# Where the squares of the input's norm stand in the first stage of a hybrid decoder block

## The chip, the cores and the metric

One core of one Trainium2 chip runs the whole kernel in one launch. The metric is the device time in microseconds (us); three runs of the kernel before give a median of 1648.81 us (1648.59 to 1650.45).

## What is computed

A decoder block of 256 tokens and 2048 channels: a mixer (gated linear attention beside causal pooling, merged by gates), a cross-attention into 256 memory tokens and a gated MLP with a causal convolution, each behind a root-mean-square norm and with a residual. All is float32. Only the start of the mixer matters here:

```python
def rms_norm(x, g):
    xf = x.astype(jnp.float32)
    y = xf * lax.rsqrt(jnp.mean(xf * xf, axis=-1, keepdims=True) + EPS)
    return (y * g.astype(jnp.float32)).astype(x.dtype)
...
    proj = h @ w_in
...
    v = heads(proj[..., OFF_V:OFF_R], GLA_HV)
...
    gate_pre = (proj[..., OFF_A:OFF_P] @ w_a2 + b_a).astype(f32)
```

where h is rms_norm(x, g_mix). The kernel multiplies by the gain first, does the products, and puts the norm's factor (one number per token) on the results.

## The kernel before

Channels lie on the partitions, in 16 chunks of 128, and the 256 tokens in the free dimension. A float32 product is made of three products of rounded operands: each operand is split in a high part (a cast to fp32r on ScalarE) and a low part (operand minus high part, on VectorE), and high x high, low x high and high x low are added up in PSUM. For weights the split is L110 (`wh`, `wl`), five buffers each, from six buffers of raw tiles that SyncE's queue loads (L78). For the input, `split_gain` (L241 to L245) scales chunk c with the gain: `h.hi(c)` on ScalarE (L243) and `h.lo(c)` on VectorE (L244).

The program begins with eight products of constants (L356), and then the projection of the values and of the decay's inputs (`va_unit`, L386 to L405). It has two halves, n = 0 (heads 0 and 1) and n = 1 (heads 2 and 3), each of six units j with 2 or 3 chunks (the table VA). For a chunk there are 2 heads x 2 halves of the tokens x 3 products (L403, L404, L405), each 260 columns wide (256 values, 4 decay inputs): 12 a chunk and 192 a half. The sums of a half stand in four PSUM tiles `va`; those of n = 0 come from the pool mm, those of n = 1 from the pool aux (four tiles each).

Transfers of the input and of the first weight pieces are issued in turn (the table FIRST, L193, and L204 to L209): chunk 0, a weight piece, chunk 1, two pieces, chunk 2, and so on; from chunk 4 on two chunks a transfer. The loop at L361 emits the splits in the same turn, and `in_order` ties each split behind the one before, so that the scheduler that orders the program keeps this sequence on ScalarE and VectorE.

The norm needs the sum of squares of each token. `Sum.add` (L262) squares a chunk on ScalarE (L265 for the first, else L260) and adds it to an accumulator (L268): even chunks to `s_mix` on VectorE, odd ones to `s_mix2` on GpSimd. The squares of a chunk are emitted one turn after its split, tied behind it (L364, L365). After the first half the two accumulators are added (L417), two products with a column of ones give the sum per token (`cols`, L274) in an aux tile of their own, `root` (L288 to L297) makes the factor `rc`, and `rows` (L277) spreads it over the partitions after unit (1, 2). `va_out` (L407) takes the results of a half out of PSUM with that factor, after each half. Calls through `behind` stand after the last product emitted so far.

Of the kernel before, what the change touches and what calls it, by code (L numbers as in the profile page):

```python
# [8 lines left out]
F32 = mybir.dt.float32  # L9
# [6 lines left out]
P = 128  # L16
# [126 lines left out]
def block(ctx, tc, xT, memT, vecs, masks, wa2, wpool, w_va, w_in, w_branch, w_out, w_ckv_k, w_ckv_v, w_cq, w_co, w_up, w_down, out):  # L143
# [11 lines left out]
    aux = ctx.enter_context(tc.tile_pool(name="aux", bufs=4, space=PS))  # L155
# [30 lines left out]
    def xc(c):  # L186
        return x[c // 4][:, c % 4, :]
# [7 lines left out]
    def in_turn(pieces):  # L195
        pieces = iter(pieces)
        for n in FIRST:
            if isinstance(n, tuple):
                yield n, None
            else:  # L200
                for _ in range(n):
                    yield None, next(pieces)
# [21 lines left out]
    def col(base, c):  # L224
        return vec[:, base + c : base + c + 1]
# [3 lines left out]
    def behind(f, *args):  # L229

        with tc.issue_after(pe["last"].ins):
            return f(*args)

    def in_order(made, f):

        with ExitStack() as stack:
            for ins in made or ():
                stack.enter_context(tc.issue_after(ins.ins))
            return f()

    def split_gain(src, act, c, base):  # L241
        return (
            nc.scalar.activation(act.hi(c), src, AF.Identity, scale=col(base, c)),  # L243
            nc.vector.scalar_tensor_tensor(act.lo(c), src, col(base, c), act.hi(c).bitcast(F32), ALU.mult, ALU.subtract),  # L244
        )  # L245
# [5 lines left out]
    class Sum:  # L251
# [15 lines left out]
            sq, a = self.square(src)  # L267
            return a, self.eng.tensor_add(self.acc, self.acc, sq)  # L268

        def cols(self):  # L270

            ps = aux.tile([P, 2], F32, tag="aux", name=f"cps_{self.name}")
            for t in range(2):
                nc.tensor.matmul(ps[:, t : t + 1], lhsT=self.acc[:, t * P : (t + 1) * P], rhs=ones[:, 0:1], start=True, stop=True)  # L274
            return root(ps, 2, self.name)
# [12 lines left out]
    def root(ps, n, name):  # L288

        v, y, z, r = (const.tile([P, n], F32, name=f"rc{i}_{name}") for i in range(4))  # L290
        nc.vector.tensor_scalar(v, ps, 1.0 / D, EPS, ALU.mult, ALU.add)
        nc.scalar.activation(y, v, AF.Sqrt)
        nc.vector.reciprocal(y, y)
        nc.vector.tensor_mul(z, y, y)
        nc.vector.scalar_tensor_tensor(z, z, -0.5, v, ALU.mult, ALU.mult)
        nc.vector.scalar_tensor_tensor(r, z, 1.5, y, ALU.add, ALU.mult)
        return r  # L297
# [13 lines left out]
    def gemm(unit, act, name, n=NC):  # L311

        ps = mm.tile([P, 2 * T], F32, tag="mm", name=f"ps_{name}")
        products(ps, terms(W.get(unit), act, n))
        return ps
# [36 lines left out]
    h = Act(big, NC, "h")  # L352

    ones_ps = aux.tile([P, P], F32, tag="aux", name="warm")
    for i in range(8):
        nc.tensor.matmul(ones_ps, lhsT=ones, rhs=ones, start=True, stop=True)  # L356


    s_mix, s_mix2 = Sum("mix"), Sum("mix2", nc.gpsimd)
    made, late = None, []  # L360
    for chunks, piece in in_turn([f for j in range(6) for f in W.pieces(va0 + j)]):  # L361
        if piece:
            made = in_order(made, piece)
        for c in late:  # L364
            in_order(made, lambda: (s_mix, s_mix2)[c % 2].add(xc(c)))  # L365
        late = range(*chunks) if chunks else ()
        for c in late:
            made = in_order(made, lambda: split_gain(xc(c), h, c, V_MIX))

    def const_loads():  # L370
        nc.sync.dma_start(mask, masks[:, 0 : N_MASK * P].rearrange("p (n i) -> p n i", i=P))
        nc.sync.dma_start(wa, wa2)

        for t in range(16):
            nc.gpsimd.memset(inv_f[:, t : t + 1], 1.0 / (t + 1))
# [8 lines left out]
    va_ps = {}  # L384

    def va_unit(n, j):  # L386

        if j == 0:
            for hd in (2 * n, 2 * n + 1):
                pool, tag = (aux, "aux") if n else (mm, "mm")  # L390
                va_ps[hd] = [pool.tile([P, 260], F32, tag=tag, name=f"va{hd}_{t}") for t in range(2)]
        wps = W.get(va0 + len(VA) * n + j)
        first, end = VA[j]
        for c in range(first, end):
            for i in range(2):
                at = 2 * (c - first) + i
                hi, lo = wps[at // (end - first)]
                at = at % (end - first) * 260
                wh, wl = hi[:, at : at + 260], lo[:, at : at + 260]
                for t in range(2):  # L400
                    ps = va_ps[2 * n + i][t]
                    xh, xl = h.hi(c)[:, t * P : (t + 1) * P], h.lo(c)[:, t * P : (t + 1) * P]
                    nc.tensor.matmul(ps, lhsT=xh, rhs=wh, start=c == 0, stop=False)  # L403
                    nc.tensor.matmul(ps, lhsT=xl, rhs=wh, start=False, stop=False)  # L404
                    pe["last"] = nc.tensor.matmul(ps, lhsT=xh, rhs=wl, start=False, stop=c == NC - 1)  # L405

    def va_out(hd):  # L407
        for t in range(2):
            ps, r = va_ps[hd][t], rc[:, t : t + 1]
            nc.scalar.activation(v[t][:, hd, :], ps[:, 0:T], AF.Identity, scale=r)  # L410
            nc.vector.tensor_scalar(a_sb[:, t, 4 * hd : 4 * hd + 4], ps[:, T : T + 4], r, None, ALU.mult)

    for n in range(2):
        for j in range(len(VA)):
            va_unit(n, j)
            if (n, j) == (0, len(VA) - 1):
                nc.vector.tensor_add(s_mix.acc, s_mix.acc, s_mix2.acc)  # L417
                rc = behind(s_mix.cols)
                const_loads()
            if (n, j) == (1, 2):  # L420
                rB = behind(s_mix.rows, rc, mm)
        for i in range(2):
            va_out(2 * n + i)

# [233 lines left out]
    for m in range(NC):  # L660
        wps = W.get(br0 + m)
        ys = []
        for n in (1, 0):
            ps = mm.tile([P, 2 * T], F32, tag="mm", name=f"br{m}_{n}")
# [34 lines left out]
    for m in range(NC):  # L699
        ps = gemm(ck0 + m, me, f"ck{m}")  # L700
# [10 lines left out]
    for g in range(4):  # L711
        acc = [mm.tile([P, 512], F32, tag="mm", name=f"cv{g}_{t}") for t in range(2)]
        for j in range(4):
            wps = W.get(cv0 + 4 * g + j)
            for k in range(4):
                hi, lo = wps[k // 2]
                wh, wl = hi[:, (k % 2) * 512 : (k % 2 + 1) * 512], lo[:, (k % 2) * 512 : (k % 2 + 1) * 512]
                c = 4 * j + k
# [11 lines left out]
    qa, ka, va, pa, pts = {}, {}, {}, {}, {}  # L730
# [58 lines left out]
    for i in range(16):  # L789
        query(i // 4, i % 4)  # L790
        hd = i // 4 - 1
# [124 lines left out]
    for m in range(NC - TAIL, NC):  # L916
        pool, tag = (aux, "aux") if m >= NC - 2 else (mm, "mm")
        ps = pool.tile([P, 2 * T], F32, tag=tag, name=f"ps_dt{m}")
# [69 lines left out]
```

## Time and profile before

| | us |
|---|---|
| median of three runs | 1648.81 |
| the profiled execution's own time | 1650.06 |
| its span | 1648.3 |
| TensorE busy in the span | 1635.4 |
| VectorE busy | 1227.9 |
| ScalarE busy | 899.4 |
| GpSimd busy | 31.1 |

The span is what the profiler saw between the first and the last instruction; the own time also holds what lies around it. PE is TensorE, DVE is VectorE, ACT is ScalarE, POOL is GpSimd, SP is SyncE, whose queue issues the transfers; a q behind the name is an engine's instruction queue. A row of a timeline begins with its start and its length in us and ends with the idle time before it and what ended that.

### The profile page before, as it was taken

How to read it: one execution, taken by the hardware profiler on the slowest of the kernel's cores; microseconds unless marked ns; L12 is line 12 of the kernel's file. 1: busy time of each engine (PE TensorE's matmuls, PEld its weight loads, DVE VectorE, ACT ScalarE, POOL GpSimd, SP SyncE). 2: the span in 40 equal slices, each digit the busy share in tenths (PEclk: the TensorE clock that was granted, in tenths of full speed). 3: DMA queues.
4: the chain of work that ended last, by engine and by line, in shares of the span. 5: the costliest groups of instructions: out<-in, count | busy, mean ns of one | idle time of the engine just before them, and what ended most of it. 6: DMA issues, size and time to landing. Idle time of an engine off the chain costs nothing.

```text
span 1648.3 us, 26006 instructions
## 1 busy us (share of the span) xinstructions
PE 1635.4 (99%) x9900; PEld 1474.9 (89%) x9900; DVE 1227.9 (74%) x1906; ACT 899.4 (55%) x1376; POOL 31.1 (2%) x137
## 2 busy tenths in 40 slices
PE   8999999999999999999999999999999999999997
PEld 8999998989988898889999999999999999999987
DVE  7588768677888855447777788886678887678876
ACT  7555447445556644446555565654356664446563
POOL 2000000000001100000000000000000000000000
PEclk9999999999999999999999999999999999999999
DMA  8665556656666666665446666666666666666663
GB/s 275 208 200 171 168 166 189 218 169 201 195 220 210 196 199 196 192 194 177 154 144 199 194 195 200 196 200 196 199 196 198 198 196 200 195 201 194 180 183 109
DMA packets 90734, 316.15 MB, mean 192 GB/s; under 512 B 10208, under 2 KB 11104, under 8 KB 90608
## 3 DMA queue, kind: packets, MB, share of 16 engines
q1 hardware_dynamic: 90464, 314.43, 61.2%
q8 instruction: 77, 1.26, 0.3%
q14 instruction: 49, 0.40, 0.1%
q10 hardware_dynamic: 144, 0.05, 0.0%
HBM read 312.35 MB, written 2.10 MB: 191 GB/s over the span
## 4 chain that ended last, share of the span: by engine, by line
PE 97%; DMA 1%; DVE 1%; ACT 1%; issue 0%; SPq 0%; DVEq 0%; ACTq 0%
PE ps_up L329 19%; PE ps_up L330 10%; PE ps_g L329 7%; PE ps_dn L329 7%; PE ps_dn L330 4%; PE ps_g L330 4%; PE ps_wc L329 3%; PE ps_ck L329 3%; PE ps_cq L329 3%; PE br L329 3%; PE ps_wo L329 3%; PE ps_cq L330 2%; PE br L330 2%; PE ps_wc L330 2%; PE ps_ck L330 2%; PE cv L722 2%
## 5 line engine op out<-in xcount | busy, mean ns | idle before, releaser
L110 ACT CAST wh<-raw 128x1024 fp32r<-128x1024 f32 (+3 forms) x602 | 613.1, 1021 | 652.4 <-issue 204.1
L110 DVE TENSOR_TENSOR wl<-raw,wh 128x1024 fp32r<-128x1024 f32 (+3 forms) x602 | 718.2, 1195 | 331.9 <-ACT wh L110 322.2
L329 PE MATMUL ps_up<-h,wh 128*128 128x512 f32 x1408 | 469.9, 380 | 0.0
L330 PE MATMUL ps_up<-h,wl 128*128 128x256 f32 x1408 | 386.4, 274 | 0.0
L329 PEld LDWEIGHTS ps_up<-h,wh 128*128 128x128 f32 x1408 | 264.3, 188 | 45.3
L330 PEld LDWEIGHTS ps_up<-h,wl 128*128 128x128 f32 x1408 | 264.5, 188 | 0.0
L329 PE MATMUL ps_g<-h,wh 128*128 128x512 f32 x512 | 173.3, 384 | 0.0
L329 PE MATMUL ps_dn<-ga,wh 128*128 128x512 f32 x512 | 170.8, 380 | 0.0
L330 PE MATMUL ps_g<-h,wl 128*128 128x256 f32 x512 | 140.6, 275 | 0.0
L330 PE MATMUL ps_dn<-ga,wl 128*128 128x256 f32 x512 | 140.5, 274 | 0.0
L329 PEld LDWEIGHTS ps_g<-h,wh 128*128 128x128 f32 x512 | 96.2, 188 | 16.8 <-ACT wh L110 0.2
L329 PEld LDWEIGHTS ps_dn<-ga,wh 128*128 128x128 f32 x512 | 96.1, 188 | 16.5
L330 PEld LDWEIGHTS ps_g<-h,wl 128*128 128x128 f32 x512 | 96.2, 188 | 0.3 <-issue 0.2
L330 PEld LDWEIGHTS ps_dn<-ga,wl 128*128 128x128 f32 x512 | 96.2, 188 | 0.0
L329 PE MATMUL ps_wo<-mg,wh 128*128 128x512 f32 x256 | 87.2, 386 | 0.1
L329 PE MATMUL ps_cq<-h,wh 128*128 128x512 f32 x256 | 86.3, 382 | 0.0
L329 PE MATMUL ps_wc<-oc,wh 128*128 128x512 f32 x256 | 85.9, 381 | 0.0
L329 PE MATMUL ps_ck<-me,wh 128*128 128x512 f32 x256 | 85.9, 382 | 0.0
L330 PE MATMUL ps_wo<-mg,wl 128*128 128x256 f32 x256 | 70.4, 276 | 0.0
L330 PE MATMUL ps_ck<-me,wl 128*128 128x256 f32 x256 | 70.3, 274 | 0.0
L330 PE MATMUL ps_cq<-h,wl 128*128 128x256 f32 x256 | 70.3, 274 | 0.0
L330 PE MATMUL ps_wc<-oc,wl 128*128 128x256 f32 x256 | 70.1, 275 | 0.0
(322 smaller groups left out, 2747.2 us busy)
## 6 DMA issues: line engine op xcount, KB each, us to landing
raw<-w_up SPq DMA_DIRECT2D x176, 512.0 KB, 4.1
raw<-w_in SPq DMA_DIRECT2D x112, 512.0 KB, 3.9
raw<-w_down SPq DMA_DIRECT2D x64, 512.0 KB, 4.3
raw<-w_branch SPq DMA_DIRECT2D x32, 512.0 KB, 4.3
raw<-w_out SPq DMA_DIRECT2D x32, 512.0 KB, 4.1
raw<-w_ckv_k SPq DMA_DIRECT2D x32, 512.0 KB, 3.9
raw<-w_ckv_v SPq DMA_DIRECT2D x32, 512.0 KB, 4.3
raw<-w_cq SPq DMA_DIRECT2D x32, 512.0 KB, 4.4
```

What stands on the lines that cost most here:

```text
L110: return self.nc.scalar.copy(hi, src), self.nc.vector.tensor_sub(lo, src, hi.bitcast(F32))
L329: nc.tensor.matmul(fours(ps), lhsT=wh, rhs=fours(act.both(c)), start=f, stop=False, skip_group_check=True)
L330: pe["last"] = nc.tensor.matmul(fours(ps[:, 0:T]), lhsT=wl, rhs=fours(act.hi(c)), start=False, stop=l, skip_group_check=True)
L722: nc.tensor.matmul(fours(acc[t]), lhsT=xh, rhs=fours(wl), start=False, stop=False)
```

## The change

The squares leave the loop that splits the input. Four of them at a time are emitted, without a tie, ahead of the units 2, 3, 4 and 5 of the first half (`mix_squares`). The column sums go to two spare columns of the first `va` tile of the first half (tiles are now 264 wide), after the first unit of the second half; that half's output follows at once, and the spread of the factor comes one unit later. There are nine products of constants in place of eight.

```diff
-        def cols(self):
+        def cols(self, ps=None):
 
-            ps = aux.tile([P, 2], F32, tag="aux", name=f"cps_{self.name}")
+            ps = aux.tile([P, 2], F32, tag="aux", name=f"cps_{self.name}") if ps is None else ps
...
-    for i in range(8):
+    for i in range(9):
         nc.tensor.matmul(ones_ps, lhsT=ones, rhs=ones, start=True, stop=True)
...
-    made, late = None, []
+    made, squared = None, [0]
     for chunks, piece in in_turn([f for j in range(6) for f in W.pieces(va0 + j)]):
         if piece:
             made = in_order(made, piece)
-        for c in late:
-            in_order(made, lambda: (s_mix, s_mix2)[c % 2].add(xc(c)))
-        late = range(*chunks) if chunks else ()
-        for c in late:
+        for c in range(*chunks) if chunks else ():
             made = in_order(made, lambda: split_gain(xc(c), h, c, V_MIX))
+
+    def mix_squares(n):
+
+        for _ in range(n):
+            c = squared[0]
+            squared[0] += 1
+            (s_mix, s_mix2)[c % 2].add(xc(c))
...
-                va_ps[hd] = [pool.tile([P, 260], F32, tag=tag, name=f"va{hd}_{t}") for t in range(2)]
+                va_ps[hd] = [pool.tile([P, 264], F32, tag=tag, name=f"va{hd}_{t}") for t in range(2)]
...
     for n in range(2):
         for j in range(len(VA)):
+            if n == 0 and j > 1:
+                mix_squares(4)
             va_unit(n, j)
             if (n, j) == (0, len(VA) - 1):
                 nc.vector.tensor_add(s_mix.acc, s_mix.acc, s_mix2.acc)
-                rc = behind(s_mix.cols)
                 const_loads()
-            if (n, j) == (1, 2):
+            if (n, j) == (1, 0):
+
+                rc = behind(s_mix.cols, va_ps[0][0][:, 260:262])
+                for hd in range(2):
+                    va_out(hd)
+            if (n, j) == (1, 3):
                 rB = behind(s_mix.rows, rc, mm)
-        for i in range(2):
-            va_out(2 * n + i)
+    for hd in range(2, 4):
+        va_out(hd)
```

What the scheduler makes of it stands in the built programs. The first instructions of ScalarE before (x_89 holds chunks 0 to 3 of the input, x_90 chunks 4 to 7, x_91 chunks 8 to 11; in brackets what an instruction waits for, DMAHW with a number being one of the eight slots of landing transfers):

```order
L243 ACTIVATE h_147<-x_89,vec 128x256 [waits DMAHW1_49,DMAHW0_49]
L110 CAST wh_0_166<-raw_0_95 128x520 [waits DMAHW2_49]
L265 ACTIVATE acc_mix<-x_89 128x256
L243 ACTIVATE h_147<-x_89,vec 128x256 [waits DMAHW3_49]
L110 CAST wh_0_166<-raw_0_95 128x260 [waits DMAHW4_49]
L265 ACTIVATE acc_mix_165<-x_89 128x256
L110 CAST wh_1_168<-raw_1_96 128x260 [waits DMAHW5_49]
```

and in the changed program:

```order
L265 ACTIVATE acc_mix<-x_89 128x256 [waits DMAHW1_49]
L265 ACTIVATE acc_mix_166<-x_89 128x256 [waits DMAHW3_49]
L260 ACTIVATE sq_mix_335<-x_89 128x256 [waits DMAHW6_49]
L260 ACTIVATE sq_mix_2_338<-x_89 128x256 [waits DMAHW0_49]
L260 ACTIVATE sq_mix_377<-x_90 128x256 [waits DMAHW2_49]
L260 ACTIVATE sq_mix_3_380<-x_90 128x256 [waits DVE_49]
L260 ACTIVATE sq_mix_383<-x_90 128x256 [waits DMAHW4_49,Pool_49]
L260 ACTIVATE sq_mix_4_386<-x_90 128x256 [waits DVE_49]
L260 ACTIVATE sq_mix_425<-x_91 128x256 [waits DMAHW6_49,Pool_49]
L243 ACTIVATE h_147<-x_89,vec 128x256
L110 CAST wh_0_167<-raw_0_95 128x520
```

Nine squares, of the chunks 0 to 8, now stand ahead of the first scaling of the input and of the first cast of a weight. The other seven stand after the cast of the ninth weight tile and of the tenth; the order on the queues of SyncE and GpSimd is the same as before. VectorE's first instructions of the changed program after its constants, where h_147 is the low part of chunk 0:

```order
L268 TENSOR_TENSOR acc_mix<-acc_mix,sq_mix_335 128x256 [waits Activation_49]
L268 TENSOR_TENSOR acc_mix<-acc_mix,sq_mix_377 128x256 [waits DVE_49,Activation_49]
L268 TENSOR_TENSOR acc_mix<-acc_mix,sq_mix_383 128x256 [waits DVE_49,Activation_49]
L268 TENSOR_TENSOR acc_mix<-acc_mix,sq_mix_425 128x256 [waits DVE_49,Activation_49]
L244 SCALAR_TENSOR_TENSOR h_147<-x_89,vec,h_147 128x256 [waits DMAHW1_49,DMAHW0_49,Activation_49]
```

Four sums now stand ahead of it; before, it was the first. On TensorE, before, the column sums stand between the halves, and the fourth tile of the second half (va_1_563) waits for VectorE to have read them:

```order
L405 MATMUL va_1_303<-wl_1_189,h_154 128x260
L274 MATMUL cps_mix<-ones,acc_mix 128x1 x2
L403 MATMUL va_0_560<-wh_0_452,h_147 128x260 [waits Activation_49]
...
L405 MATMUL va_0_562<-wl_0_453,h_147 128x260
L403 MATMUL va_1_563<-wh_0_452,h_147 128x260 [waits DVE_49]
```

and in the changed program after the 36 products of the second half's first unit, into the first half's first tile:

```order
L409 MATMUL va_1_543<-wl_1_444,h_148 128x260
L274 MATMUL va_0_257<-ones,acc_mix 128x1 x2
L407 MATMUL va_0_540<-wh_0_489,h_148 128x260 [waits Activation_49]
L408 MATMUL va_0_540<-wh_0_489,h_148 128x260
L409 MATMUL va_0_540<-wl_0_490,h_148 128x260 [waits DVE_49]
```

No product of the second half waits for the reading of the column sums any more.

## Rows read from the trace of the kernel before

**Rows 1.** The page, part 1: busy us of each engine, share of the span.

```profile
PE 1635.4 (99%) x9900; PEld 1474.9 (89%) x9900; DVE 1227.9 (74%) x1906; ACT 899.4 (55%) x1376; POOL 31.1 (2%) x137
```

**Rows 2.** TensorE's longest wait after 36 us; then the stretch 40 to 100 us.

```profile
PE rps_fin L909 <- DVE diag_fin L907: 1.7, 1, 1.7
...
40.00:100.00 60.00, 60.00 (x396) 55.20 (x396) 41.44 (x69) 35.05 (x45) 0.00 (x0) 1.00 0.65 213
```

**Rows 3.** Timeline of TensorE, 1 to 58 us.

```profile
1.22 3.58 PE L356 MATMUL warm<-ones 128*128 128x128 f32 x16 [1.22 <-DVE ones L219]
4.81 0.39 PE L403 MATMUL va<-wh,h 128*128 128x260 f32 x1
...
5.55 0.40 PE L405 MATMUL va<-wl,h 128*128 128x260 f32 x1
...
12.00 0.29 PE L403 MATMUL va<-wh,h 128*128 128x260 f32 x1
...
16.09 0.28 PE L404 MATMUL va<-wh,h 128*128 128x260 f32 x1
...
19.58 0.39 PE L405 MATMUL va<-wl,h 128*128 128x260 f32 x1 [0.67 <-DVE wl L110]
...
32.39 0.50 PE L274 MATMUL cps_mix<-ones,acc_mix 128*128 128x1 f32 x4
32.76 0.36 PE L403 MATMUL va<-wh,h 128*128 128x260 f32 x1
...
34.67 0.39 PE L403 MATMUL va<-wh,h 128*128 128x260 f32 x1 [0.59 <-DVE rc_mix L291]
...
57.18 0.38 PE L329 MATMUL ps_k<-h,wh 128*128 128x512 f32 x1
```

**Rows 4.** Timeline of ScalarE, 4 to 22 us.

```profile
4.14 0.62 ACT L110 CAST wh<-raw 128x520 fp32r<-128x520 f32 x1 [0.37 <-DMA raw<-w_va]
...
9.09 0.41 ACT L260 ACTIVATE sq_mix<-x 128x256 f32<-128x256 f32 x1
9.41 0.49 ACT L243 ACTIVATE h<-x,vec 128x256 fp32r<-128x256 f32 x1
9.87 0.84 ACT L110 CAST wh<-raw 128x780 fp32r<-128x780 f32 x1
...
20.35 0.84 ACT L110 CAST wh<-raw 128x780 fp32r<-128x780 f32 x1 [2.72 <-DMA raw<-w_va]
21.10 0.91 ACT L243 ACTIVATE h<-x,vec 128x256 fp32r<-128x256 f32 x2
```

**Rows 5.** VectorE's second low part of a weight; line L268 (ns min/median/max).

```profile
5.92 0.42 DVE L110 TENSOR_TENSOR wl<-raw,wh 128x260 fp32r<-128x260 f32 x1
...
L268 DVE TENSOR_TENSOR acc_mix<-acc_mix,sq_mix x7: 409/419/970, 9.8 to 29.5; 128x256 f32<-128x256 f32 x7
L268 POOL TENSOR_TENSOR acc_mix<-acc_mix,sq_mix x7: 771/1000/1466, 11.1 to 27.9; 128x256 f32<-128x256 f32 x7
```

**Rows 6.** Input transfers: chunks 8 and 9; all ten; the seventh weight tile, from the chain.

```profile
7.87 0.33 SPq L209 DMA_DIRECT2D x<-xT  x1
...
DMA to landing us min/median/max: 6.3/6.3/6.3
...
L209 SPq DMA_DIRECT2D x<-xT x10: 328/426/631, 0.7 to 10.7; - x10
...
DMA to landing us min/median/max: 2.3/6.0/6.8
...
12.56 7.71 DMA raw<-w_va
```

**Rows 7.** Two products of TensorE near the end; the stretch 1643 to 1644 us (eighth column PEclk).

```profile
1633.11 0.48 PE L909 MATMUL rps_fin<-diag_fin,ones 128*128 128x128 f32 x2
1633.35 5.07 PE L928 MATMUL ps_dt<-ga,wh 128*128 128x256 f32 x41
...
1643.00:1644.00 1.00, 0.00 (x0) 0.00 (x0) 1.00 (x3) 0.00 (x0) 0.00 (x0) 0.50 0.29 111
```

More of the change, by code (lines that the diff above doesn't have):

```diff
@@ L400, in va_unit @@
                 for t in range(2):
-                    ps = va_ps[2 * n + i][t]
+                    ps = va_ps[2 * n + i][t][:, 0:260]
                     xh, xl = h.hi(c)[:, t * P : (t + 1) * P], h.lo(c)[:, t * P : (t + 1) * P]
```

## The prediction

> **What bounds the kernel now.** I read the page first, then the waits of TensorE, then the first 60 us engine by engine. TensorE is busy for 1635.4 of 1648.3 us [rows 1]. After the first 36 us the longest of its three waits for another engine is 1.7 us, in the last 10 us of the program, and a stretch such as 40 to 100 us is filled without a gap [rows 2]. So a microsecond that TensorE loses or gains before 36 us arrives whole at the end; nothing later can swallow it.
>
> The first 57 us are the value projection: two halves (heads 0 and 1, then 2 and 3) of 192 products each, 16 chunks of the input by 2 heads by 2 halves of the tokens by 3 terms. From 12.00 to 16.09 us 34 products follow each other without a hole, 0.1203 us apart [rows 3], so a half needs 23.10 us. The first half took from 4.81 to 32.39, that is 27.58 us: 4.48 us were lost to late inputs, for instance 0.67 us before 19.58, where the low part of a weight tile was late on VectorE. The second half took from 32.76 to 57.18, 24.42 us, with 0.59 us lost before 34.67 to the norm's column sums (their bank was still being read) [rows 3].
>
> **The change, part by part.**
>
> *The squares.* On paper the squares of four chunks stand ahead of units 2 to 5. They are no longer tied to their neighbours, and the built program has nine of the sixteen (chunks 0 to 8) at the very head of ScalarE's queue, ahead of the first scaling of chunk 0, and four sums at the head of VectorE's. That the queue is served in its order the trace shows: ScalarE sat idle 2.72 us until 20.35, waiting for a weight tile, while the scaling behind it (21.10) was waiting for nothing: all ten transfers of the input start by 10.7 us and need at most 6.8, so its chunks had landed by 17.5 [rows 4, 6]. Now the last of the nine squares needs chunk 8. Its transfer is issued at 7.87 us and takes 6.3 [rows 6], and the order on SyncE's queue is unchanged, so it lands at 14.17 as before. From there: one square, 0.32 us to the next instruction (9.09 to 9.41); the scaling of chunk 0, 0.46 to the next (9.41 to 9.87); the cast of the first weight piece and the start of TensorE, 0.67 (4.14 to 4.81) [rows 3, 4]. The first product of the projection starts at 14.17 + 0.32 + 0.46 + 0.67 = **15.62** and not at 4.81.
>
> The other eight squares are early and cost nothing in themselves: they run in the gaps between landings. For chunk 8's square a buffer must be given back by GpSimd's sum of chunk 5, at most 1.47 us [rows 5]; chunk 5 shares chunk 4's transfer, issued two before chunk 8's, so that sum is most likely over by 14.17, and at worst it adds its 1.47. VectorE's fourth sum (0.42 [rows 5]) runs beside the scaling on ScalarE, and the low part of chunk 0 needs that scaling anyway; zero, at worst 0.42.
>
> *After the start.* TensorE has the first product that needs the low weights 0.74 us after its first (4.81 to 5.55) [rows 3]; I keep that: 16.36. 189 products are left, 22.74 us if nothing else is late. I count none of the 4.48 us lost before as coming back: by 16 us all input is there, two chunks cost TensorE 24 x 0.1203 = 2.89 us, and ScalarE and VectorE need for them two scalings (0.9) and some 1040 weight columns (about 1.1 to 1.3, from 0.83 for 780), about 2 us each [rows 4]; they draw ahead. The weight tiles are later too: the seventh needs the buffer of the first, which VectorE gave back with the second low part at 5.92 + 0.42 = 6.34, 2.20 us after the first cast began at 4.14 [rows 4, 5]. That cast now begins at 14.95, so the buffer is free at 17.15, where SyncE issued at 12.56 before. Landing took 7.71 us then [rows 6]; that gives 24.9 now. TensorE wants it after 108 products, at 16.36 + 105 x 0.1203 = 29 or later. Its cast and low part take about 2 us more. Hidden, with 2 us to spare; were the transfer slower by more than that, TensorE would wait for the rest.
>
> *The clock.* TensorE would have nothing to do from about 5 to 15.6 us. At the end of the program, after a few scattered products, the granted clock is 0.50 (1.2 GHz) from 1643 to 1644 [rows 7]. So I expect the restart at 1.2 GHz. What that costs: the 16 first warming products take 3.58 us, 0.22 each; two of the same shape near the end take 1633.11 to 1633.35, 0.12 each [rows 3, 7]. The ratio is 1.87 (the clock view prints 1.00 for that first stretch, but the spacing is that of the slow level). Each slow microsecond loses 0.465 us. The bounds: none slow, 0; twice as long as the warming row, (7.16 - 0.74) x 0.465 = 2.99. I take the row itself, (3.58 - 0.74) x 0.465 = **1.32**, the only restart that this trace holds. The Trainium skill, TensorE: Matmul & The Clock Gate, section What's actually happening, says that the number of slow products at a start varies from run to run for one kernel and names 6, 11 and 14. By those counts, at 0.105 us lost for each product here, my estimate is 0.6 to 1.5 us in place of 1.32, and a time of 1655.5 to 1656.4; no run here shows the spread yet.
>
> *The column sums.* They cost 0.37 us of TensorE (32.39 to 32.76 [rows 3]) wherever they stand, now after the first unit of the second half. Their own bank is gone, so the 0.59 us before 34.67 goes: the second half takes 24.42 - 0.59 = 23.83. What then is late next is the norm itself and the first half's output, a unit later; the banks they free are wanted only by the row sums, one unit later too, and at 57 us. Zero; if the wait stays in another form, 0.59 is back.
>
> *The ninth warming product* adds 3.58 / 8 = 0.45 us at most, inside the idle stretch before 15.62: zero. Four more columns in the tile move nothing.
>
> *Sum.* 15.62 + 0.74 + 22.74 + 1.32 = 40.42; + 0.37 + 23.83 = 64.62 for the end of the projection, against 57.18: **7.44 us later**. The profiled execution took 1650.06, 1.76 around its span of 1648.3; its own sum is 1657.5. The median of the three runs is 1648.81, so I say 1648.81 + 7.4 = **1656.2**.
>
> **The rivals.**
>
> *The late start is followed by late inputs as before.* If the 4.48 us of the first half are lost again behind the wait: 1656.2 + 4.5 = 1660.7. For it: VectorE has wait after wait of TensorE on its side. Against it: those losses fell while inputs were landing, and by 16 us they have.
>
> *The head of the queue does not hold, and the kernel gains.* The mechanism: with the squares and sums out of the first two units ScalarE and VectorE cast and split earlier, and TensorE's waits for low weights (0.67 at 19.58) and for the bank (0.59) go: 1648.8 - 1.3 = 1647.5; were all 4.48 and 0.59 to go, 1643.7. It decides at the first product: with 7.44 us in hand the break-even is a start at 8.2 us. For that chunk 8 must land by 6.7; its transfer is not issued before 7.87. That speaks against it as strongly as a row can, unless the order that runs is not the one built.
>
> *The hold is short and nothing measurable comes of it.* Chunk 8 lands early by some 5 us, and slow start and gains even out near 1649. Against it: the order and the sizes of the transfers ahead of it are what they were, and ScalarE's waiting does not speed them.
>
> **How the numbers follow.** About 0.2%, 3.3 us, is what a measurement of this kernel tells from no change. Forecast 0.82, more lost inputs 0.08, the gain 0.05 (of it 0.02 beyond 3.3 us), the short hold 0.05 (slower by over 3.3 us in 0.02 of it). So slower 0.92, same 0.06, faster 0.02. The range: without a slow clock 7.44 - 1.32 = 6.1, with the longest and the 0.59 left in, 7.44 + 1.67 + 0.59 = 9.7; the three runs lie from 1648.59 to 1650.45, so a median may move by 1 either way: 1653.9 to 1659.5, taken as 1653.7 to 1659.5.
>
> **What would show it.** Right: ScalarE's first nine entries are squares, with idle time until transfers of the input, the last at about 14.2; a hole in TensorE from 5 to 15.6; a granted clock of 0.5 in it and for some 3 us after; no hole from there to 57 + 7 us; no wait of TensorE for the norm's first step. Wrong: a first product before 10 us; a clock that never falls (1.3 us less); holes after 17 us (a later end by their sum); any later stretch, from 65 us on, that takes less time than before.

## The result, and the profile after

The changed kernel takes **1659.5 us** (median of four runs, 1658.64 to 1660.17); the kernel before took 1648.83 beside it (median of four, 1648.59 to 1650.45). The ratio is 1.0059 with an interval of 1.0047 to 1.0070: slower by 7.7 to 11.5 us. The forecast was slower, by 7.4 us, with a range that ends at 1659.5: the median lies on its upper edge.

The profiled execution took 1658.64 us, its span is 1656.9, against 1650.06 and 1648.3 before. The busy times have hardly moved from [rows 1]; TensorE's has grown by 0.8 us, so nearly all of the loss is idle time. The page, part 1, of the changed kernel:

```profile
PE 1636.2 (99%) x9902; PEld 1476.5 (89%) x9902; DVE 1225.4 (74%) x1906; ACT 901.7 (54%) x1376; POOL 30.5 (2%) x137
```

The waits of the changed kernel, first 90 us (the engine and line that waited, what for, us in all, times, the longest):

```profile
PE va L407 <- ACT wh L110: 10.8, 1, 10.8
...
ACT sq_mix L260 <- DMA x<-xT: 6.0, 4, 2.2
```

In the projection TensorE waits once, 10.8 us, for the first cast of a weight; its other waits in this stage, before the change 1.2 us for low weights, 0.9 for a cast and 0.6 for the column sums, are gone. ScalarE, whose cast it is, waits meanwhile for the input with its squares. Its timeline, from the first square to the first cast:

```profile
3.21 0.42 ACT L265 ACTIVATE acc_mix<-x 128x256 f32<-128x256 f32 x1 [0.55 <-DMA x<-xT]
...
11.41 0.72 ACT L260 ACTIVATE sq_mix<-x 128x256 f32<-128x256 f32 x2 [2.21 <-DMA x<-xT]
13.16 0.72 ACT L260 ACTIVATE sq_mix<-x 128x256 f32<-128x256 f32 x2 [1.02 <-DMA x<-xT]
14.81 0.42 ACT L260 ACTIVATE sq_mix<-x 128x256 f32<-128x256 f32 x1 [0.93 <-POOL acc_mix L268]
15.13 0.49 ACT L243 ACTIVATE h<-x,vec 128x256 fp32r<-128x256 f32 x1
15.53 0.61 ACT L110 CAST wh<-raw 128x520 fp32r<-128x520 f32 x1
```

Two squares start as chunks 4 and 5 land, two with 6 and 7, and the ninth, chunk 8's, at 14.81; 0.72 us later the first cast begins. The scaling of chunk 0 at 15.13 waited for nothing but its turn. TensorE, whose products before the change began at 4.81 and ended at 57.18 [rows 3]:

```profile
1.22 4.21 PE L356 MATMUL warm<-ones 128*128 128x128 f32 x18 [1.22 <-DVE ones L219]
16.19 0.59 PE L407 MATMUL va<-wh,h 128*128 128x260 f32 x1 [10.77 <-ACT wh L110]
...
17.01 0.51 PE L409 MATMUL va<-wl,h 128*128 128x260 f32 x1
...
20.77 0.38 PE L409 MATMUL va<-wl,h 128*128 128x260 f32 x1
20.99 0.28 PE L407 MATMUL va<-wh,h 128*128 128x260 f32 x1
21.11 0.28 PE L408 MATMUL va<-wh,h 128*128 128x260 f32 x1
...
45.89 0.50 PE L274 MATMUL va<-ones,acc_mix 128*128 128x1 f32 x4
...
65.49 0.38 PE L329 MATMUL ps_k<-h,wh 128*128 128x512 f32 x1
```

Up to 20.99 the products stand 0.217 us apart, but for two steps of 0.38 and 0.30; from there 0.120. None of the rows after the first product's shows a wait. The projection ends 65.49 - 57.18 = 8.31 us later; what follows takes 1656.9 - 65.49 = 1591.4 us where it took 1648.3 - 57.18 = 1591.1. So of the 8.6 us between the two profiles all but 0.3 was made before 65.49.

### The profile page after: what moved, and what is told of

The parts are those of the page before. It is cut to its first block, busy times and chain, and to the rows that moved or that the text cites. A ratio compares the mean times of both kernels' runs of the same rounds, so it can differ in the third digit from the quotient of the medians.

```text
span 1656.9 us, 26013 instructions
## 1 busy us (share of the span) xinstructions
PE 1636.2 (99%) x9902; PEld 1476.5 (89%) x9902; DVE 1225.4 (74%) x1906; ACT 901.7 (54%) x1376; POOL 30.5 (2%) x137
## 4 chain that ended last, share of the span: by engine, by line
PE 98%; DMA 0%; SPq 0%; DVE 0%; ACT 0%; issue 0%; DVEq 0%; ACTq 0%
PE ps_up L329 19%; PE ps_up L330 10%; PE ps_g L329 7%; PE ps_dn L329 7%; PE ps_g L330 4%; PE ps_dn L330 4%; PE ps_wc L329 3%; PE ps_ck L329 3%; PE ps_cq L329 3%; PE ps_wo L329 3%; PE br L329 3%; PE ps_cq L330 2%; PE ps_wc L330 2%; PE br L330 2%; PE ps_ck L330 2%; PE cv L731 2%
```

## The experiments

My theory: nine untied squares at the head of ScalarE's queue hold the scalings and casts behind them until chunk 8 lands; all else in the change is worth less than can be measured. The rivals: the loss comes from the other half of the change (column sums, output a unit later); or from the clock; or from the squares' work wherever it stands. The runs stand in three groups, each on a chip of its own and with its own runs of the kernel before, which is why the ratios are given: 1650.63 (21 runs, 1648.59 to 1651.96) for tied, only_squares, only_sums and warm54; 1649.07 (30 runs, 1646.89 to 1652.48) for four_free, behind_all, two_squares and sums_vec; 1649.00 (21 runs, 1647.04 to 1651.22) for the last three.

**The kernel before with the squares' part of the change alone.** The loop over the chunks loses its squares, and `mix_squares` is called as in the change; column sums and output stay.

```diff
-        for c in late:
-            in_order(made, lambda: (s_mix, s_mix2)[c % 2].add(xc(c)))
...
+            if n == 0 and j > 1:
+                mix_squares(4)
             va_unit(n, j)
```

> The kernel before with the untied squares alone; column sums, outputs and the eight constant products as before. If the hold is the cause: first product at 16.2 us, as slow as the change or up to 0.6 us slower: 1659 to 1660.5. If the moved column sums and outputs are the cause: 1649.

1659.03 us (five runs, 1656.84 to 1659.55), ratio 1.0053 (1.0040 to 1.0065). TensorE's first product and the clock by stretches (length, busy times, the granted clock last but two, DMA share, GB/s):

```profile
16.12 0.58 PE L407 MATMUL va<-wh,h 128*128 128x260 f32 x1 [11.16 <-ACT wh L110]
```

```profile
5.00:16.00 11.00, 0.00 (x0) 0.00 (x0) 2.09 (x5) 3.86 (x11) 2.16 (x3) 0.65 0.96 336
16.00:21.00 5.00, 4.88 (x22) 4.86 (x23) 4.97 (x12) 5.00 (x12) 0.00 (x0) 0.50 0.53 143
21.00:40.00 19.00, 19.00 (x157) 19.00 (x157) 14.91 (x26) 13.94 (x28) 4.87 (x5) 0.98 0.77 239
```

The squares alone are 8.4 us slower than the kernel before beside them, as much as the change within the two intervals: they make the loss. This execution recorded the fall of the clock: it falls within the idle stretch, is 0.50 (1.2 GHz) from 16 to 21 us and comes back soon after. In the changed kernel's own profile the clock column prints 1.00 for these stretches, with the same spacing of 0.217 us.

**The other part alone**: nine products of constants, column sums in the spare columns, output after unit (1, 0).

```diff
...
-                rc = behind(s_mix.cols)
                 const_loads()
-            if (n, j) == (1, 2):
+            if (n, j) == (1, 0):
+                rc = behind(s_mix.cols, va_ps[0][0][:, 260:262])
+                for hd in range(2):
+                    va_out(hd)
+            if (n, j) == (1, 3):
...
```

> The change with the squares left where they were before: column sums in spare columns, first half's output and the spread moved, nine constant products. If the hold is the cause: the kernel before less the wait of 0.59 us, plus or minus nothing else: 1648.0 to 1648.6. If the moved sums and outputs are the cause: near 1659.

1650.41 us (11 runs, 1648.76 to 1651.40), ratio 1.0001 (0.9992 to 1.0010). The projection ends at 55.89, 1.3 us before that of the kernel before, and TensorE's 0.59 us for the column sums [rows 3] is gone from its waits, but so little can't be told in the median. The 1648.0 to 1648.6 that I expected are missed, since the kernel before itself stood at 1650.63 beside it and the median is only 0.2 under that. This half is worth nothing measurable and costs nothing measurable: the first rival falls.

**The changed kernel with the squares tied** behind the splits of units 2, 3, 4 and 5 (`mades` collects what the loop ties).

```diff
...
+            mades.append(made)
...
-                mix_squares(4)
+                in_order(mades[3 + 2 * j], lambda: mix_squares(4))
```

> The change with one thing undone: each group of four squares is tied behind the split of the last weight piece of its unit, so that no square stands ahead of the first scaling. If the hold at the head of ScalarE's queue is the cause, the first product is back at about 4.8 us and the whole 10.7 us go. What is left of the change can then save the 0.59 us of the bank and little more, since the seventh weight tile lands at 20.35 us whatever ScalarE does before it; sums that wait for GpSimd could hold the last weight tiles of the half by up to 1 us. So 1647.5 to 1649.8. If the moved column sums and outputs are the cause, it stays near 1659; if late weight tiles are, in between.

1653.53 us (11 runs, 1651.50 to 1654.68), ratio 1.0017 (1.0008 to 1.0026); the first product starts at 5.08 and the projection ends at 58.96. The hold is undone, but the 1647.5 to 1649.8 us that I expected are missed by 3.7; half of that is the kernel before, which stood 1.8 us higher beside these runs than where I took it from. TensorE's holes in the tied kernel:

```profile
29.10 0.39 PE L410 MATMUL va<-wl,h 128*128 128x260 f32 x1 [0.46 <-DVE wl L110]
30.93 0.39 PE L408 MATMUL va<-wh,h 128*128 128x260 f32 x1 [0.37 <-ACT wh L110]
31.84 0.39 PE L410 MATMUL va<-wl,h 128*128 128x260 f32 x1 [0.41 <-DVE wl L110]
33.61 0.39 PE L408 MATMUL va<-wh,h 128*128 128x260 f32 x1 [0.30 <-ACT wh L110]
35.17 0.39 PE L410 MATMUL va<-wl,h 128*128 128x260 f32 x1 [1.05 <-DVE wl L110]
```

and ScalarE at the same time:

```profile
29.95 0.42 ACT L260 ACTIVATE sq_mix<-x 128x256 f32<-128x256 f32 x1 [1.01 <-DVE acc_mix L268]
30.27 0.61 ACT L110 CAST wh<-raw 128x520 fp32r<-128x520 f32 x1
...
32.41 0.42 ACT L260 ACTIVATE sq_mix<-x 128x256 f32<-128x256 f32 x1 [0.60 <-POOL acc_mix L268]
32.73 3.81 ACT L110 CAST wh<-raw 128x780 fp32r<-128x780 f32 x5
```

With sixteen squares in some ten microseconds these holes are 2.6 us in all. By the releasers that the timeline names, ScalarE waits there for sums that hold the three buffers of the squares, and the five casts at 32.73 stand behind. Whether the buffers are the cause is tried at the end.

**The changed kernel with 54 products of constants in place of nine**, so that TensorE is busy while it waits.

```diff
-    for i in range(9):
+    for i in range(54):
```

> The changed kernel with 54 constant products in place of 9, so that TensorE is busy until some 15 us. If the restart at 1.2 GHz costs what the spacing of products says (4.8 us at 0.217 us a product against 0.120, that is 2.1 us in the profiled execution, more in the others whose clock was lower), the first products follow at 0.12 us from 16.2 us on, the time falls by 2 to 3.2 us to 1656.3 to 1657.5, and the runs scatter less. If the clock costs nothing here because the inputs are late anyway, it stays at 1659.5.

1657.89 us (five runs, 1656.28 to 1658.49), ratio 1.0046 (1.0033 to 1.0058). TensorE:

```profile
1.22 13.85 PE L356 MATMUL warm<-ones 128*128 128x128 f32 x108 [1.22 <-DVE ones L219]
16.00 0.39 PE L407 MATMUL va<-wh,h 128*128 128x260 f32 x1 [0.93 <-ACT wh L110]
...
16.95 0.28 PE L407 MATMUL va<-wh,h 128*128 128x260 f32 x1
17.07 0.28 PE L408 MATMUL va<-wh,h 128*128 128x260 f32 x1
```

The products stand 0.12 us apart from the start, but for a wait of 0.23 us for a low weight. The projection ends at 63.56, 1.93 us before the changed kernel's; 0.19 of it is the earlier start, the rest, 1.7, is what the slow clock costs in the end. The hold itself, some 6.4 us, stays: the clock is a part of the loss, not its cause. The median is 1.6 us below the changed kernel's, short of the 2 to 3.2 that I expected, and 1.1 below that of only_squares on the same chip, with intervals that overlap; so it is the profile that shows the clock's price, not the median.

**Four free squares only**: chunks 0 to 3 untied, the other twelve tied as in the tied kernel.

```diff
...
-                mix_squares(4)
+                in_order(mades[3 + 2 * j] if j > 2 else None, lambda: mix_squares(4))
```

> The changed kernel with only the first four squares (chunks 0 to 3) left untied, the other twelve tied behind the units 3, 4 and 5. If the hold is as long as the landing of the last untied chunk, it ends with chunk 3 near 8.8 us and the first product starts near 10.2 in place of 4.8 and 16.2. Half of that delay should not arrive, since the seventh weight tile lands at 19 to 20.4 us either way: the projection ends at 58 to 61 us, the time is 1 to 4 us over the kernel before, far less than half of the change's loss. If the loss is not a matter of which chunk is waited for, it stays near 1659 or falls to that of the tied kernel.

1652.75 us (eight runs, 1650.34 to 1653.88), ratio 1.0026 (1.0016 to 1.0037). ScalarE's last free square and TensorE's first product:

```profile
8.21 0.42 ACT L260 ACTIVATE sq_mix<-x 128x256 f32<-128x256 f32 x1 [1.36 <-DMA x<-xT]
```

```profile
9.60 0.58 PE L408 MATMUL va<-wh,h 128*128 128x260 f32 x1 [4.17 <-ACT wh L110]
```

The start follows the landing of the last free square's chunk: chunk 3 in place of chunk 8, 9.60 in place of 16.19. The projection ends at 58.8, 1.6 us after the kernel before. TensorE has no hole after its start, so nearly all of the kernel before's 4.48 us is covered. The two doses give the exchange: 6.59 us of start are 6.7 us at the end, and, extrapolated at that rate, the end is that of before for a start at 9.60 - 1.6 = 8.0 us.

**All squares late**: in the kernel with the column sums' change, all sixteen tied behind the last split of the first half.

```diff
...
-                mix_squares(4)
+                in_order(made, lambda: mix_squares(4))
```

> The change with all sixteen squares tied behind the last split of the first half. The tied kernel ended its projection 1.8 us later than the kernel before, with 2.4 us of TensorE waiting for low weights in the last units. Theory: the squares stand in a bunch that is paced by the sums (VectorE, GpSimd) and holds the casts and low parts behind it; then the bunch now holds the second half's first weight tiles instead, the waits move to 30 to 37 us and the time is that of the tied kernel within 1 us (1.5 to 4 over before). Rival: the waits in the tied kernel come from weight transfers; then they stay where they were, and the time is that of the kernel before less 0.6.

1648.89 us (11 runs, 1646.99 to 1651.46), ratio 0.9999 (0.9990 to 1.0009). This misses what I expected: the bunch costs next to nothing there. The projection ends at 56.1, 1.0 us before that of the kernel before. After 13 us the timeline names one wait of TensorE:

```profile
32.34 0.39 PE L410 MATMUL va<-wl,h 128*128 128x260 f32 x1 [0.60 <-DVE wl L110]
```

The casts of the first half stand ahead of the squares, and TensorE has their products to do meanwhile. So sixteen squares at once are nearly free behind the casts, where the tied kernel, with the squares between them, was 2.9 us slower than the kernel before.

**What is there to gain?** The tied kernel with the squares of chunks 0 and 1 alone:

```diff
...
-                mix_squares(4)
+                in_order(mades[3 + 2 * j], lambda: mix_squares(2 if j == 2 else 0))
```

> The tied kernel with the squares and sums of the chunks 2 to 15 left out, so that the norm is made of two chunks alone. It bounds what moving the squares could ever bring. If the squares and sums delay TensorE in the kernel before, the 4.48 us that its first half loses come back and the time is 4 to 5 us under before. If the landing of the first weight tiles and of the seventh (19 to 20.4 us) sets the first half, only the bank's 0.59 and some tenths come back: 0.5 to 1.5 us under before.

1648.42 us (11 runs, 1646.25 to 1649.82), ratio 0.9995 (0.9987 to 1.0004). The projection ends at 54.9 in this profile, 2.3 us before [rows 3], and the median shows no difference. What stays late is a weight tile; ScalarE, with hardly a square to do, still sits:

```profile
10.47 0.84 ACT L110 CAST wh<-raw 128x780 fp32r<-128x780 f32 x1 [1.87 <-DMA raw<-w_va]
```

That is the third tile. TensorE's last wait in the projection ends at 12.37; the seventh tile, whose cast begins at 18.97, makes none, so of the two landings that I had named only the early ones are left as a limit.

**The column sums' change with a transfer out of the way**: the late vectors' transfer, which stands between weight tiles on SyncE's queue, is issued after the first half.

```diff
-    nc.sync.dma_start(vec[:, V_CB:], vecs[:, V_CB:])
...
+        tc.keep_in_program_order(nc.sync.dma_start(vec[:, V_CB:], vecs[:, V_CB:]))
```

> The kernel with only the column sums and outputs moved, and in addition the transfer of the late vectors (L210, 180 KB) issued after the constants of the first half in place of ahead of the seventh weight tile. If the landing of that tile sets the first half, it lands some 0.5 us earlier and the projection ends up to 0.5 us earlier than the 55.9 of the kernel with the sums alone; the time 0.3 to 1.5 us under before, the best of all so far. If not, it equals the kernel with the sums alone.

1648.72 us (11 runs, 1647.52 to 1650.49), ratio 0.9995 (0.9987 to 1.0004): no measurable gain. In the profile the cast of the seventh tile begins at 18.95, where it began at 19.06 with the sums alone, and the projection ends at 56.62, 0.7 us later and not earlier. But here TensorE, after waits of 1.21 and 0.50 us up to 12.55, ran at half the clock for a while, as the stretch shows (columns as above):

```profile
13.00:16.50 3.50, 3.50 (x19) 3.50 (x18) 3.50 (x7) 3.50 (x9) 1.32 (x3) 0.51 1.04 402
```

At 0.097 us more for each of some 16 products that is about 1.6 us (an estimate from the spacings 0.217 and 0.120), so this profile can't tell whether the transfer matters. None of the versions beats the kernel before by more than its scatter.

**What released the ninth square?** The timeline names GpSimd's sum at 14.81. But the program has three buffers, so that square needs the buffer of chunk 5, and GpSimd's sum of chunk 5 was over by 13.0; the one that ended just then (14.02 + 0.72 = 14.74) was chunk 7's. The transfer of chunks 8 and 9 in the changed kernel, with its time to landing:

```profile
L209 SPq DMA_DIRECT2D x<-xT x1: 663/663/663, 7.1 to 7.1; - x1
...
DMA to landing us min/median/max: 7.7/7.7/7.7
```

It landed at 7.07 + 7.7 = 14.8 (7.07 is its row in SyncE's timeline). To tell the two apart, the changed kernel with five buffers for the squares (the same edit stands at the four other tiles of this tag):

```diff
-            sq = sm.tile([P, T], F32, tag="sq", name=f"sq_{self.name}_{self.n}", bufs=3)
+            sq = sm.tile([P, T], F32, tag="sq", name=f"sq_{self.name}_{self.n}", bufs=5)
```

> The changed kernel with five buffers for the squares in place of three (so chunk 8's square needs the buffer of chunk 3, whose sum ends near 10.0 us, and no longer that of chunk 5); the order on every engine is the same. Theory: the square of chunk 8 waits for its own transfer, which the changed kernel's trace issues at 7.07 us and lands 7.7 us later, at 14.8; then nothing moves: that square starts at 14.6 to 15.0 and the first product of the projection at 16.0 to 16.4, the time stays at 1657 to 1660.5. Rival: it is GpSimd's sum that holds the buffer, as the timeline names it; then the square starts as soon as the chunk is there, which this rival puts at 14.17 as in the kernel before, the first product at 15.5 to 15.7, and the time falls by 0.6 us, which only the profile can tell.

1656.49 us (four runs, 1655.78 to 1657.22), ratio 1.0047 (1.0033 to 1.0060). ScalarE's ninth square and, for the same transfer, the landing:

```profile
14.41 0.42 ACT L260 ACTIVATE sq_mix<-x 128x256 f32<-128x256 f32 x1 [1.00 <-DMA x<-xT]
```

```profile
L209 SPq DMA_DIRECT2D x<-xT x1: 709/709/709, 7.0 to 7.0; - x1
...
DMA to landing us min/median/max: 7.3/7.3/7.3
```

The square starts as its chunk lands, 0.4 us earlier than in the other profile because the landing was earlier by as much (all the landings were: the pair of chunks 4 and 5 at 11.01 in place of 11.41). 14.41 is below the 14.6 to 15.0 that I wrote down, since I took one execution's landing for all; and since the landing moved, this run alone does not part the two. What parts them is the landing at 14.8 and the order of the buffers: in both kernels the square starts when its chunk has landed, and in the changed kernel the sum that it could have needed was over 1.8 us before. So the landing holds the queue, not the buffer. The time is 3.0 us below the changed kernel's. Of the 2.4 us between the two profiles 0.3 stands at the end of the projection and 1.6 in one later stage (the last section has it); what makes the rest is not shown.

**The tied kernel with five buffers** (the edit is that of the run above), **and the tied kernel again beside it.**

> The tied kernel (squares tied behind the splits of units 2 to 5) with five buffers for the squares in place of three; the order on every engine is the same. Theory: the bunch costs because a square waits for a buffer that a sum on GpSimd or VectorE still holds (1.8 us of ScalarE's idle time between 28 and 33 us in the tied kernel), with the casts queued behind it; with five buffers those waits go, TensorE's five holes after 29 us (2.6 us in sum) shrink to under 1 us, the projection ends at 56.5 to 57.5 us and the time is 1 to 3 us below that of the tied kernel. Rival: the bunch costs by its sheer work on ScalarE and VectorE in these microseconds; the holes stay above 2 us, and the time is that of the tied kernel within 1 us.

> The tied kernel once more beside the one with five buffers, on the same chip: 1651.5 to 1654.7 us as before, holes of TensorE after 29 us of 2 to 3 us in sum.

With five buffers 1651.31 us (11 runs, 1649.64 to 1652.86), ratio 1.0016 (1.0007 to 1.0025); with three 1651.52 (11 runs, 1649.37 to 1652.28), ratio 1.0012 (1.0003 to 1.0021). TensorE with five buffers:

```profile
28.56 0.39 PE L410 MATMUL va<-wl,h 128*128 128x260 f32 x1 [0.47 <-DVE wl L110]
31.45 0.39 PE L410 MATMUL va<-wl,h 128*128 128x260 f32 x1 [1.18 <-DVE wl L110]
34.27 0.39 PE L410 MATMUL va<-wl,h 128*128 128x260 f32 x1 [1.11 <-DVE wl L110]
```

Three holes of 2.76 us in place of five (2.6, and 2.5 in the kernel run again), and the same time. More buffers let ScalarE run ahead, but then VectorE, with the sums between its low parts, is what TensorE waits for. My theory falls, and the rival's figures came: the bunch costs by the work it puts between casts and low parts. This work is more than its own length, though. Two low parts of VectorE and GpSimd's sums, with five buffers:

```profile
22.96 0.69 DVE L110 TENSOR_TENSOR wl<-raw,wh 128x520 fp32r<-128x520 f32 x1
30.18 1.21 DVE L110 TENSOR_TENSOR wl<-raw,wh 128x520 fp32r<-128x520 f32 x1
```

```profile
26.94 5.06 POOL L268 TENSOR_TENSOR acc_mix<-acc_mix,sq_mix 128x256 f32<-128x256 f32 x5 [0.40 <-ACT sq_mix L260]
```

The same operation on VectorE takes 0.69 us while GpSimd is idle and 1.05 (at 27.46) and 1.21 beside GpSimd's sums. How much of the holes is this slowing and how much the squares and sums themselves, no run separates.

## Why the prediction was right

**The mechanism** is the one forecast, step by step: nine squares first on ScalarE, a hole in TensorE from the end of its constants to the first cast, a restart at the slow spacing, no hole after that, no wait for the norm's sums, later stages as before. only_squares shows that the squares' place alone makes the loss, four_free that its size follows the chunk that is waited for. Of the rivals, late inputs again did not come (no wait of TensorE after 17 us), chunk 8 did not land early, and the start was far beyond the break-even that the gain needed, given as 8.2 us; the doses, extrapolated, put it at 8.0.

**The sizes**, in the profiled execution. The end of the projection was forecast at 64.62 and came at 65.49, 0.87 later:

- The start: 15.62 forecast, 16.19 measured, +0.57. The step that failed is that chunk 8 lands at 14.17 "as before". SyncE issued its transfer earlier, at 7.07 in place of 7.87 [rows 6], yet it took 7.7 us in place of 6.3 and landed at 14.8 (14.4 in after_five). From there the chain of 0.32, 0.46 and 0.67 came as 0.32, 0.40 and 0.66. Here the time of a transfer was not its own: with the DMA engines busy at a share of 0.97 from 5 to 16 us before and of 0.99 after, an issue 0.8 us earlier bought no earlier landing. In only_squares, after_five and four_free, issued at 7.0 to 7.1 too, it landed at 14.1 to 14.6; what makes the difference is open.
- Low weights and the clock: 0.74 - 3 x 0.1203 + 1.32 = 1.70 forecast. Measured, the first 21 products take 20.99 - 16.19 = 4.80 us; at 0.1203 each they are 2.53, so 2.27, +0.57. By the spacing, 21 x (0.217 - 0.120) = 2.0 of it is the clock and some 0.2 the low weights, so it is the clock's term, 1.32, that was too small: the warming row, the only restart in the trace, was too short. The Trainium skill, TensorE: Matmul & The Clock Gate, section What's actually happening, warns that the count of slow products varies between runs and names 6, 11 and 14; here 21 were slow. That the count varies the runs bear out (21 also in four_free, 26 in only_squares); the estimate made from its figures, up to 1.5 us, was below the 2.0 measured.
- The second half: its 23.83 us hold 0.73 beyond 192 x 0.1203, and 0.37 stands for the sums, 1.10 in all. From 45.89 to 65.49 there are 19.60 us, of which 156 products take 18.77: 0.83, so -0.27. The bank's 0.59 us went as forecast.

The three make 0.87. Around this the terms that I called zero were zero: the ninth constant product (its row ends at 5.43, with 10.77 us idle behind it), the output a unit later, the weight tiles issued later.

**The median** is 10.7 us above that of before, where the two profiles differ by 8.6: the profiled execution of before lies 1.2 us above its median, that of the changed kernel 0.9 below. The other three runs of the changed kernel have spans of 1657.5 to 1658.4, 0.6 to 1.5 above the profiled one. That is inside what executions of one kernel differ by (the kernel before spans 5.6 us over 30 runs). Of the kernels with the same hold only_squares is 8.4 above its runs of before, after_five 7.5. The forecast of +7.4 fits those better than it fits 10.7; how much of it is the changed kernel's own can't be told from four runs. That the median still lies in the range, on its very edge, is luck in part: the range reached so far up by 0.59 us for a wait that was gone and by 1 us for scatter.

## What to carry to other kernels

Look at what stands ahead of the first cast in an in-order queue: work that nobody waits for yet, left without a tie, may be put at its head, and then each piece of it holds everything behind it until its own transfer lands. A late start is not lost whole (here about 3 us of it, by the break-even above, were had back from inputs that had arrived meanwhile), so count the start against the losses that it covers. Moving fill-in work as a bunch was free here only behind the casts that feed the bound engine; among them it cost 2.3 to 2.9 us, with three buffers or five.

## What the runs showed of the hardware

- **One kernel's stages run at two paces**, without a wait that shows. Of two executions of the tied kernel, on two chips, the stage of ps_wo takes 87.3 us in the first and 85.7 in the second (tied_again), with the granted clock printed as 1.00. Their 512-column products (durations, min/median/max):

```profile
L329 PE MATMUL ps_wo<-mg,wh x256: 380/387/494, 475.3 to 562.2; 128*128 128x512 f32 x128
```

```profile
L329 PE MATMUL ps_wo<-mg,wh x256: 380/380/496, 474.8 to 560.2; 128*128 128x512 f32 x128
```

  387 ns or 380 for the median product, 1.6 us for the stage. The stage of ps_wc has it the other way round, 92.3 us in the first and 93.8 in the second, so it is not a faster and a slower chip. The changed kernel and after_five differ in ps_wo by the same 87.3 and 85.7. In the profile of warm54 ps_wc too took the slower pace, 93.9 us, which hides most of its 1.9 us gain there. The cause is open. It may be a part of why the kernel before ranges from 1646.89 to 1652.48 over 30 runs, whose stages no profile shows.
- **The pace at the program's start differs from execution to execution** as well. The same two executions of the tied kernel, TensorE's first products:

```profile
5.08 0.57 PE L408 MATMUL va<-wh,h 128*128 128x260 f32 x1
5.44 0.42 PE L409 MATMUL va<-wh,h 128*128 128x260 f32 x1
5.66 0.42 PE L408 MATMUL va<-wh,h 128*128 128x260 f32 x1
5.88 0.42 PE L410 MATMUL va<-wl,h 128*128 128x260 f32 x1
```

```profile
5.50 0.39 PE L410 MATMUL va<-wl,h 128*128 128x260 f32 x1
5.72 0.28 PE L409 MATMUL va<-wh,h 128*128 128x260 f32 x1
5.84 0.28 PE L410 MATMUL va<-wl,h 128*128 128x260 f32 x1
```

  In the first they stand 0.217 us apart until 6.7, the spacing that stood beside a granted clock of 0.50 (1.2 GHz) in only_squares; in the second (tied_again) 0.12 nearly from the start. Both come after the same nine products of constants, and the clock column prints 1.00 for both.
- **A named releaser can be a coincidence.** The wait at 14.81 was put down to a GpSimd sum that ended 0.07 us before; the order of the buffers and the landing time pointed to the transfer, and with five buffers the square again started as its chunk landed.
